# Expert gate and up products: weights become the stationary operand, 96 token slots stream, high and low halves lie side by side

## The chip, the core and the metric

The kernel runs as one launch on one core of a Trainium2 chip. The metric is the device time of that launch in microseconds (us). Below, PE is TensorE's matrix multiply, PEld its weight load, DVE VectorE, ACT ScalarE, POOL GpSimd, SP SyncE, whose queue issues the large transfers.

## The reference

Two transformer blocks over 256 tokens of 1024 features. The part that matters here is the last layer's mixture of experts: 8 experts of 3584 hidden features, the best two for each token.

```python
def moe_swiglu(t, router, w_gate, w_up, w_down):
    logits = (t @ router).astype(jnp.float32)
    top_logits, top_idx = lax.top_k(logits, TOP_K)
    gates = jax.nn.softmax(top_logits, axis=-1)
    combine = jnp.sum(jax.nn.one_hot(top_idx, N_EXPERTS, dtype=jnp.float32) * gates[..., None], axis=1)
    out = jnp.zeros_like(t)
    for e in range(N_EXPERTS):
        out = out + combine[:, e:e + 1].astype(t.dtype) * swiglu(t, w_gate[e], w_up[e], w_down[e])
    return out
```

`swiglu` is silu(t wg) * (t wu), then times wd. For the inputs that the reference draws, its own routing gives the 8 experts 67, 89, 50, 69, 56, 58, 78 and 45 tokens.

## The kernel before

Every f32 operand is split into a high part (rounded to float32r) and a low part (what is left), and a product is the sum of three matmuls: high by high, high by low, low by high (`mm3`, L522 to L524). `load_w` (L494) fetches a weight tile in transfers of 1 MB into buffers `wf`, 12 of them in rotation, and splits it in units of 128 x 1024: ACT casts the high part `wh` (L491), DVE subtracts to get the low part `wl` (L492). `wh` and `wl` have four buffers each.

`moe` (L1623) routes first: each token gets a slot among an expert's tokens, up to 128 slots, and `G` is the one-hot matrix from tokens to slots. `gather` (L1713) multiplies the tokens by `G` for two experts at a time and leaves `xh` and `xl`, features on partitions, 2 x 128 slots on the free axis. Then come 8 experts with 7 chunks of 512 hidden features each. A chunk is `gate_up` (L1761) and, one chunk later, `down` (L1779):

- `gate_up` makes two products, gate and up, with `tm`: the 128 slots are the stationary operand (a 128 x 128 piece of `xh` or `xl` for each of 8 feature tiles), and 512 weight columns stream. That is 2 x 8 x 3 = 48 matmuls of 512 columns, into PSUM tiles `mm` of one bank, four in rotation. ACT takes silu of the gate sums (L1767), DVE multiplies by the up sums (L1768). The result has slots on partitions; four transposes on PE (L1771) turn it, ACT and DVE split it into `eah` and `eal` (L1775, L1776).
- `down` streams 512 columns of wd against `eah` and `eal`, 4 x 2 x 3 = 24 matmuls, into two banks `dn` that accumulate over the expert's 7 chunks.

After an expert's last chunk `combine` (L1792) weights its rows and returns them to their tokens. `finish` then takes the final norm and writes the output. `overflow` (L1821) computes slots 128 and up again in a loop that is entered only when an expert has more than 128 tokens.

The order on each engine is set by a scheduler when the program is built. All of `wf`'s transfers are issued by SP, in the order in which the tiles are used.

Of the kernel before, what the change touches and what calls it, by code (L numbers as in the profile page):

```python
# [9 lines left out]
F32 = mybir.dt.float32  # L10
F32R = mybir.dt.float32r
AF = mybir.ActivationFunctionType
OP = mybir.AluOpType
# [10 lines left out]
MLA_STEPS = 1.4  # L24
MODS_F32 = (1,3,5)
# [123 lines left out]
class Rwkv:  # L149
    """The recurrent mixer: r, k, v, feature-major [P, 4, S] (two heads a tile); chunks of 64 tokens."""  # L150
# [26 lines left out]
    def decays(self):  # L177
        """Decay from the start of a chunk of 64 tokens: to the token (e0), to the one before it (e1), inverted (em)."""
# [21 lines left out]
    def removal(self):  # L200
        """Normalized removal key."""
# [12 lines left out]
    def keys(self):  # L214
        """k (1 + (a - 1) k_a); decayed removal and replacement keys."""
# [15 lines left out]
    def blocks(self):  # L231
        """Diagonal blocks of 16 x 16, to one block per partition."""
# [27 lines left out]
    def inverses(self):  # L260
        """Inverses of the diagonal blocks by forward substitution, and back to tokens on partitions."""
# [20 lines left out]
    def queries(self):  # L282
        """Decayed queries and keys; bonus."""
# [26 lines left out]
    def group(self, g, yt):  # L310
        """Heads 4g .. 4g + 3, all tokens; a generator of steps."""
# [12 lines left out]
        for tt in range(2):  # L324
# [3 lines left out]
            # token-major copies  # L328
# [15 lines left out]
            # inverse of the 64 x 64 blocks, transposed  # L344
# [38 lines left out]
            # the two chunks of 64 tokens  # L383
# [33 lines left out]
    def finish(self, j, yt):  # L417
        """Group norm, bonus, gate of head pair j."""
# [14 lines left out]
class Build:  # L433
# [60 lines left out]
    def load_w(self, src, kt, cols):  # L494
        """Loads and splits a weight tile [P, kt, cols]; a list of (k0, kn, hi, lo) units."""
# [30 lines left out]
    def fm(self, units, c0, act, t0, n, M=P):  # L526
        """Feature-major product: weight columns c0..c0+M on partitions, tokens t0.. on the free axis."""
# [7 lines left out]
    def side(self, ws, act, ns):  # L535
        """Feature-major products of several weight tiles side by side, so that each uses act as it comes."""
# [9 lines left out]
    def tm(self, units, c0, n, act, t0):  # L546
        """Token-major product: tokens t0..t0+127 on partitions, weight columns c0.. on the free axis."""
# [37 lines left out]
    def head_rstd(self, sq, n, eps, floor=None):  # L585
        """1/sqrt(sum of sq over the 64 features of a head + eps), [P, n] in PSUM, for sq of two heads."""
# [18 lines left out]
    def spread(self, out, cols):  # L605
        """Token-major columns as rows, the same on every partition."""
# [4 lines left out]
    def first_rstd(self, h):  # L611
        """The same of the two inputs, in SBUF, for a start with nothing else to do."""
# [11 lines left out]
    def modnorm(self, h, act, streams, gs, sh, rs=None, first=None):  # L624
        """act = split(rmsnorm(h)*gs + sh); gs, sh: per stream [P, KT] columns (sh None: no shift)."""
# [20 lines left out]
    # ------------------------------------------------------------------ block 1  # L646
# [25 lines left out]
    def mods(self, l, chunks, plain=()):  # L672
        """Modulation vectors of layer l, columns in chunks of 384, both streams, feature-major; one step a chunk."""
# [68 lines left out]
    def gains(self, l, which, name):  # L742
        """Per stream (norm gain * (1 + scale)) and shift columns."""
# [11 lines left out]
    def decay(self, l, h, cross):  # L755
        """Transposed decay matrix [keys, queries] of retention head h, keys and queries of one stream or across."""
# [19 lines left out]
    def softmax_pv(self, scores, nkt, vt, opart, ops, ocols):  # L776
        """scores: one [P queries, nkt*P keys] tile per query tile; o^T (64 rows) goes into ops."""
# [19 lines left out]
    def padded(self, src, par, n):  # L797
        """One head's rows of a head pair's [P, n] tile, the other head's rows zero."""
# [35 lines left out]
    def rot(self, ps, dst, scale):  # L834
        """dst = scale * rotary(ps) for a [P, S] tile of two heads' features."""
# [9 lines left out]
    def retention(self, l, hp, rq, rk, rv, gate, ns):  # L845
        """Head pair hp: normalized, gated output replaces gate."""
# [28 lines left out]
    def headnorm(self, ops, n, eps, narrow=False):  # L875
        """(y - mean) / sqrt(var + eps) per head of 64 features, of a [P, n] PSUM tile of two heads."""
# [21 lines left out]
    def neighborhood(self, l, hp, naq, nak, nav, out, ns):  # L898
        """Head pair hp: output goes to out."""
# [35 lines left out]
    def layer_a(self, l):  # L935
# [111 lines left out]
        # output projection, gated residual  # L1047
# [5 lines left out]
        # convolutional feed-forward  # L1053
# [16 lines left out]
        for half in range(2):  # L1070
# [9 lines left out]
            for ft in range(0, KT, 2):  # L1080
                # two tiles side by side at first, while the last products are split
# [10 lines left out]
    def conv(self, l, ps, f, ns):  # L1092
        """Depthwise convolution over tokens of one feature tile, with bias."""
# [24 lines left out]
    def raw(self):  # L1118
        """The next buffer for weights as they come: the weight pool's, then those that another pool adds."""
# [38 lines left out]
    def leave(self):  # L1158
        """Block 1's output hb = rmsnorm(h) * g, and 1/rms of hb (from the mean squares of h * g)."""
# [37 lines left out]
    # ------------------------------------------------------------------ block 2  # L1197
    def norm_into(self, dst, name, then=lambda k: None):
        """dst = rmsnorm(h) * gain, f32."""
        rs = self.rstd(self.h, KT, S, self.c("mean"), self.eps, 0)  # L1200
        for k in range(KT):
            self.nc.vector.scalar_tensor_tensor(dst[:, k, :S], self.h[:, k, :S], self.v(name, k), rs[:, :S],
# [3 lines left out]
    def attention(self, q, k, v, opart, ops, scale):  # L1206
        """Causal attention of one head over S tokens: q, k [rows, S] feature-major, v(kt) [P, 64] token-major."""
# [26 lines left out]
    def layer_b0(self, rs=None, enter=None, leave=None):  # L1234
# [78 lines left out]
        # the shared rotary key, once per quadrant  # L1313
# [22 lines left out]
    def last(self, g):  # L1336
        """Runs a generator to its end; its value."""
# [6 lines left out]
    def rounds(self, *parts):  # L1344
        """Steps of (generator, steps a round), interleaved until all have ended."""
# [10 lines left out]
    def out_proj(self, w_out, yt, k0):  # L1356
        """Adds the products of mixer outputs k0 .. k0 + 3 to h; a generator."""
# [34 lines left out]
    def rope(self, ps, swap, cos, sin, writes, scale=1.0):  # L1392
        """Rotary embedding of a [P, S] tile; writes: (destination, rows)."""
# [10 lines left out]
    def mla(self, wqn, wqr, wkv, ql, kvl, kpe, yt):  # L1404
# [26 lines left out]
        # heads 0, 1 of a group: rotary rows in 0-63, the rest in rows 64-127; heads 2, 3 the other way round  # L1431
# [39 lines left out]
    def layer_b1(self, rs):  # L1471
# [14 lines left out]
        # on the side where weights of the experts come early, once the first heads are done  # L1486
# [13 lines left out]
        # forget gates: inclusive cumulative log-sigmoid, one head per partition  # L1500
# [17 lines left out]
        # extra rows of a head's keys and queries: D[query] * 1 + 1 * (-D[key])  # L1518
# [29 lines left out]
        def pair(kt, q, k, v, scale):  # L1548
            """Attention of two heads, in step; their outputs split."""
# [38 lines left out]
        def routing(k):  # L1588
            """Squares and router logits of feature tile k, summed token-major; the norm's factor comes later."""
# [33 lines left out]
    def moe(self, sums, copies):  # L1623
# [30 lines left out]
        # token-major copies of the normalized tokens  # L1654
# [337 lines left out]
```

## Time and profile before

| what | value |
|---|---|
| time, median of 3 runs | 2738.32 us (2736.84 to 2741.67) |
| span of the profiled execution, from the first to the last instruction | 2735.8 us |
| the experts' stage in it, first product to last (1710.2 to 2715.2) | 1005 us |
| PE, DVE, ACT, POOL busy, share of the span | 97%, 73%, 60%, 7% |
| HBM read | 581.82 MB |

The profile is one execution, taken by the hardware profiler. It names instructions by line and by tiles, out<-in; a PE row's first tile after the arrow is the operand that streams. A matmul's row runs from its start to its modelled end, and successive matmuls overlap, so the distance between two starts says more than a duration. The profile gives no time for its own execution but the span, which lies 2.5 us below the median of the runs.

### The profile page before, as it was taken

What the parts mean: (1) busy time and instruction counts of PE and PEld (TensorE: products, weight loads), DVE (VectorE), ACT (ScalarE), POOL (GpSimd) and SP (SyncE); (2) the same over time, 40 slices, a digit from 0 to 9 for tenths busy, and PEclk for the clock granted to TensorE, in tenths of its full rate; (3) what the DMA queues carried; (4) which work ended last, traced back from release to release, by engine and by line L of the source; (5) the groups of instructions that cost most, each with busy time, mean ns of one, the idle gap of its engine ahead of it and who ended that gap; (6) DMA issues with size and microseconds to landing.
All of it is one profiled execution on the core that took longest, in us unless ns stands there. A gap on an engine that the chain in (4) does not pass through costs nothing.

```text
span 2735.8 us, 39494 instructions
## 1 busy us (share of the span) xinstructions
PE 2667.3 (97%) x14922; PEld 2206.9 (81%) x14922; DVE 1985.2 (73%) x2920; ACT 1632.5 (60%) x2459; POOL 202.7 (7%) x247
## 2 busy tenths in 40 slices
PE   7999999999999999999999999999999999999998
PEld 3866677888887799987899988888887787788776
DVE  5366668557455687675655568999989888888886
ACT  4365555334345665565444465877777777777775
POOL 0112100000112200222010100000000000000000
PEclk9999999999999999999999999999999999999998
DMA  7245245435241455531255546899999999999992
GB/s 260 74 149 173 86 130 193 133 130 167 93 134 47 129 180 192 168 122 25 86 174 197 182 140 238 309 367 353 326 358 346 362 334 364 343 360 332 365 345 100
DMA packets 113876, 585.93 MB, mean 214 GB/s; under 512 B 19537, under 2 KB 23137, under 8 KB 68753
## 3 DMA queue, kind: packets, MB, share of 16 engines
q1 hardware_dynamic: 111296, 575.57, 59.2%
q0 software_dynamic: 2384, 7.79, 1.1%
q8 instruction: 119, 1.95, 0.3%
q14 instruction: 77, 0.62, 0.1%
HBM read 581.82 MB, written 1.47 MB: 213 GB/s over the span
## 4 chain that ended last, share of the span: by engine, by line
PE 62%; DVE 2%; ACT 2%; DMA 1%; issue 1%; POOL 0%; DVEq 0%; ACTq 0%; SPq 0%; POOLq 0%
PE mm L523 14%; PE mm L522 14%; PE mm L524 14%; PE dn L522 4%; PE dn L523 4%; PE dn L524 4%; PE sm L169 1%; PE sm L1771 1%; DVE wl L492 1%; PE sm L1721 1%; ACT wh L491 0%; PE sm L1211 0%; DMA wf<-moe_wd 0%; PE sm L1227 0%; DMA wf<-ffn_wg 0%
## 5 line engine op out<-in xcount | busy, mean ns | idle before, releaser
L492 DVE TENSOR_TENSOR wl<-wf,wh 128x1024 fp32r<-128x1024 f32 (+3 forms) x1254 | 1288.5, 1056 | 396.8 <-ACT wh L491 387.2
L491 ACT CAST wh<-wf 128x1024 fp32r<-128x1024 f32 (+3 forms) x1254 | 1104.9, 907 | 587.9 <-PE mm L523 347.7
L522 PE MATMUL mm<-ah,wh 128*128 128x256 f32 (+1 forms) x1768 | 573.0, 328 | 12.3 <-ACT ah L642 5.9
L524 PE MATMUL mm<-ah,wl 128*128 128x256 f32 (+1 forms) x1768 | 571.4, 324 | 1.8 <-DVE wl L492 1.6
L523 PE MATMUL mm<-al,wh 128*128 128x256 f32 (+1 forms) x1768 | 570.2, 323 | 0.0
L522 PEld LDWEIGHTS mm<-ah,wh 128*128 128x128 f32 x1768 | 335.0, 191 | 46.3 <-ACT ah L642 7.0
L524 PEld LDWEIGHTS mm<-ah,wl 128*128 128x128 f32 x1768 | 336.6, 191 | 32.7 <-DVE wl L492 3.7
L523 PEld LDWEIGHTS mm<-al,wh 128*128 128x128 f32 x1768 | 337.2, 191 | 31.0 <-issue 4.6
L523 PE MATMUL mm<-wl,xh 128*128 128x512 f32 x896 | 358.1, 400 | 2.0 <-DVE wl L492 2.0
L522 PE MATMUL mm<-wh,xh 128*128 128x512 f32 x896 | 355.9, 397 | 0.0
L524 PE MATMUL mm<-wh,xl 128*128 128x512 f32 x896 | 353.5, 395 | 0.0
L523 PEld LDWEIGHTS mm<-wl,xh 128*128 128x128 f32 x896 | 168.5, 188 | 51.9 <-DVE wl L492 13.1
L522 PEld LDWEIGHTS mm<-wh,xh 128*128 128x128 f32 x896 | 168.6, 188 | 38.8
L524 PEld LDWEIGHTS mm<-wh,xl 128*128 128x128 f32 x896 | 168.4, 188 | 37.5
L524 PE MATMUL dn<-wh,eal 128*128 128x512 f32 x448 | 180.7, 403 | 0.0
L523 PE MATMUL dn<-wl,eah 128*128 128x512 f32 x448 | 177.7, 397 | 0.0
L522 PE MATMUL mm<-gh,wh 128*128 128x256 f32 (+1 forms) x528 | 169.2, 320 | 0.0
L523 PE MATMUL mm<-gl,wh 128*128 128x256 f32 (+1 forms) x528 | 169.1, 320 | 0.0
L524 PE MATMUL mm<-gh,wl 128*128 128x256 f32 (+1 forms) x528 | 169.1, 320 | 0.0
L522 PE MATMUL dn<-wh,eah 128*128 128x512 f32 x448 | 158.1, 397 | 0.0
L524 PEld LDWEIGHTS mm<-gh,wl 128*128 128x128 f32 x528 | 100.2, 190 | 8.0
L523 PEld LDWEIGHTS mm<-gl,wh 128*128 128x128 f32 x528 | 100.2, 190 | 7.9
(514 smaller groups left out, 3422.0 us busy)
## 6 DMA issues: line engine op xcount, KB each, us to landing
wf<-moe_wg SPq DMA_DIRECT2D x112, 1024.0 KB, 6.8
wf<-moe_wu SPq DMA_DIRECT2D x112, 1024.0 KB, 6.8
wf<-moe_wd SPq DMA_DIRECT2D x112, 1024.0 KB, 6.4
wf<-w_mod SPq DMA_DIRECT2D x64, 768.0 KB, 4.4
wf<-w_up SPq DMA_DIRECT2D x88, 512.0 KB, 3.5
wf<-w_down SPq DMA_DIRECT2D x32, 704.0 KB, 4.0
wf<-w_out SPq DMA_DIRECT2D x32, 512.0 KB, 3.9
wf<-w_qkg SPq DMA_DIRECT2D x30, 512.0 KB, 3.5
```

The source lines that it names most:

```text
L169: self.nc.tensor.matmul(o, l, r, start=True, stop=True)
L491: nc.scalar.copy(dh, src)
L492: nc.vector.tensor_tensor(dl, src, dh.bitcast(F32), op=OP.subtract)
L522: nc.tensor.matmul(out, lh, rh, start=first, stop=False)
L523: nc.tensor.matmul(out, lh, rl, start=False, stop=False)
L524: nc.tensor.matmul(out, ll, rh, start=False, stop=last)
L1721: nc.tensor.matmul(ps[:, m * S:m * S + S], src[:, tt, k * P:k * P + P], G[:, tt, e0:e0 + 2], start=tt == 0, stop=tt == 1)
L1771: nc.tensor.transpose(ps[:, j * P:j * P + P], s[:, j * P:j * P + P], self.c("ident"))
```

## The change

`SLOTS = 96` replaces 128 as the number of slots of an expert. In `gate_up` the operands change places: a 128 x 128 piece of the weights, `wh` or `wl`, is loaded as the stationary operand, and slots stream. `gather` now leaves one tile `xg` for each of the two experts, with 96 high columns and 96 low columns side by side, so a matmul with `wh` streams all 192 columns and one with `wl` the 96 high ones. The high and low sums are added afterwards (ACT copies one half, DVE adds the other). The sums have hidden features on partitions, so no transposes follow. A product's `mm` tile has two banks now, and there are two such tiles instead of four of one bank. `gather` for the next pair of experts is called at chunk 3 of the odd expert instead of its last chunk, into three `xg` buffers. `down` and `combine` are cut to 96 partitions. `overflow` runs for slots from 96 and from 224, each behind a test of its own.

```diff
-        self.psum((4, 2))
+        self.psum((2, 2))
...
         def gather(e0):
-            xh = self.mk(mp, [P, KT, S], F32R, "xh")
-            xl = self.mk(mp, [P, KT, S], F32R, "xl")
+            xs = [self.mk(mp, [P, KT, 2 * SLOTS], F32R, "xg", 3) for _ in range(2)]
+            n = 2 * SLOTS
             for k in range(KT):
                 ps = self.smps()
                 for m, src in enumerate((th, tl)):
                     for tt in range(2):
-                        nc.tensor.matmul(ps[:, m * S:m * S + S], src[:, tt, k * P:k * P + P], G[:, tt, e0:e0 + 2],
+                        nc.tensor.matmul(ps[:, m * n:m * n + n], src[:, tt, k * P:k * P + P], G[:, tt, e0:e0 + 2],
                                          start=tt == 0, stop=tt == 1)
-                nc.scalar.copy(xh[:, k], ps[:, :S])
-                nc.vector.tensor_copy(xl[:, k], ps[:, S:])
-            return xh, xl
+                v = ps[:, :2 * n].rearrange("p (m e c) -> p e m c", m=2, e=2)
+                for i, (x, copy) in enumerate(zip(xs, (nc.scalar.copy, nc.vector.tensor_copy))):
+                    copy(x[:, k].rearrange("p (m c) -> p m c", m=2), v[:, i])
+            return xs
...
-                a = self.gate_up(mp, e, ch, x, (e % 2) * P)
-                if e % 2 and ch == NC - 1 and e + 1 < E:
+                a = self.gate_up(mp, e, ch, x[e % 2])
+                if e % 2 and ch == 3 and e + 1 < E:
                     nx = gather(e + 1)
...
-    def gate_up(self, mp, e, ch, x, c0):
+    def gate_up(self, mp, e, ch, x):
         nc, I = self.nc, self.I
         TT = nc.vector.tensor_tensor
-        pg = [self.tm(self.load_w(I[n][e, ch], KT, 512), 0, 512, x, c0) for n in ("moe_wg_1_2", "moe_wu_1_2")]
-        s = self.t2k()
-        nc.scalar.activation(s, pg[0], AF.Silu)
-        TT(s, s, pg[1], op=OP.mult)
-        ps = self.smps()
-        for j in range(4):
-            nc.tensor.transpose(ps[:, j * P:j * P + P], s[:, j * P:j * P + P], self.c("ident"))
-        ah = self.mk(mp, [P, 4, P], F32R, "eah", 2)
-        al = self.mk(mp, [P, 4, P], F32R, "eal", 2)
-        p3 = ps.rearrange("p (j t) -> p j t", j=4)
-        nc.scalar.copy(ah, p3)
-        TT(al, p3, ah.bitcast(F32), op=OP.subtract)
+        n = 2 * SLOTS
+        sums = []
+        for name in ("moe_wg_1_2", "moe_wu_1_2"):
+            pg = self.mk(self.ps, [P, 2, 512], F32, "mm", 2)
+            for k0, kn, wh, wl in self.load_w(I[name][e, ch], KT, 512):
+                for i in range(kn):
+                    k = k0 + i
+                    for j in range(4):
+                        o = pg[:, j // 2, j % 2 * n:j % 2 * n + n]
+                        f = slice(j * P, j * P + P)
+                        nc.tensor.matmul(o, wh[:, i, f], x[:, k], start=k == 0 and j % 2 == 0, stop=False,
+                                         skip_group_check=True)
+                        nc.tensor.matmul(o[:, :SLOTS], wl[:, i, f], x[:, k, :SLOTS], start=False, stop=k == KT - 1,
+                                         skip_group_check=True)
+            v = pg[:, :, :2 * n].rearrange("p b (j h c) -> p b j h c", j=2, h=2)
+            t = self.t2k()[:, :4 * SLOTS]
+            t4 = t.rearrange("p (b j c) -> p b j c", b=2, j=2)
+            nc.scalar.copy(t4, v[:, :, :, 1])
+            TT(t4, v[:, :, :, 0], t4, op=OP.add)
+            if not sums:
+                nc.scalar.activation(t, t, AF.Silu)
+            sums.append(t)
+        s = sums[0]
+        TT(s, s, sums[1], op=OP.mult)
+        ah = self.mk(mp, [P, 4, SLOTS], F32R, "eah", 2)
+        al = self.mk(mp, [P, 4, SLOTS], F32R, "eal", 2)
+        s3 = s.rearrange("p (j t) -> p j t", j=4)
+        nc.scalar.copy(ah, s3)
+        TT(al, s3, ah.bitcast(F32), op=OP.subtract)
         return ah, al
...
     def overflow(self, mp, cnti, pos, sel, comb, th, tl, finish):
+        n = self.nc.values_load(cnti[0:1, 0:1], min_val=0, max_val=S)
+        for first in range(SLOTS, S, P):
+            self.overflow_part(mp, n, first, pos, sel, comb, th, tl, finish)
```

On PE, before, this stands where a chunk's down products end and the next chunk's gate product begins (a matmul's first name is where it adds, the two behind the arrow are the operands, the size is that of the result):

```order
L522 MATMUL dn_17099<-wh_17554,eah_17388 128x512
L523 MATMUL dn_17099<-wl_17555,eah_17388 128x512
L524 MATMUL dn_17099<-wh_17554,eal_17389 128x512
L522 MATMUL mm_17602<-wh_17584,xh_16799 128x512
L523 MATMUL mm_17602<-wl_17585,xh_16799 128x512
L524 MATMUL mm_17602<-wh_17584,xl_16800 128x512
```

And this stands at the same kind of place now:

```order
L523 MATMUL dn_18883<-wh_19636,eah_19332 96x512
L524 MATMUL dn_18883<-wl_19637,eah_19332 96x512
L525 MATMUL dn_18883<-wh_19636,eal_19333 96x512
L1779 MATMUL mm_19664<-xg_16800,wh_19667 128x192
L1781 MATMUL mm_19664<-xg_16800,wl_19668 128x96
L1779 MATMUL mm_19664<-xg_16800,wh_19667 128x192
L1781 MATMUL mm_19664<-xg_16800,wl_19668 128x96
L1779 MATMUL mm_19664<-xg_16800,wh_19667 128x192
L1781 MATMUL mm_19664<-xg_16800,wl_19668 128x96
```

Three matmuls of 512 columns for each of 8 feature tiles have become eight of 192 and 96 columns in turn, 64 for a product; the down products keep their count and their 512 columns, and the order of gate, up and down is kept.

On ACT, before, this stands where the gate sums of a chunk are read (`wh` rows are the casts of weights, the last four here those of a down tile):

```order
L491 CAST wh_18269<-wf_18263 128x1024
L1767 ACTIVATE t2k_18298<-mm_18228 128x512
L491 CAST wh_18312<-wf_18310 128x1024
L491 CAST wh_18316<-wf_18310 128x1024
L491 CAST wh_18322<-wf_18320 128x1024
L491 CAST wh_18326<-wf_18320 128x1024
```

And now, from the casts of the up tile to those of the next chunk's gate tile:

```order
L492 CAST wh_19540<-wf_19538 128x1024
L492 CAST wh_19544<-wf_19538 128x1024
L1786 COPY t2k_19523<-mm_19438 128x384
L1789 ACTIVATE t2k_19523<-t2k_19523 128x384
L492 CAST wh_19622<-wf_19620 128x1024
L492 CAST wh_19626<-wf_19620 128x1024
L492 CAST wh_19632<-wf_19630 128x1024
L492 CAST wh_19636<-wf_19630 128x1024
L1786 COPY t2k_19612<-mm_19527 128x384
L492 CAST wh_19667<-wf_19665 128x1024
```

The gate sums are still read behind the last cast of the up tile; what is new is a copy of the up sums, which stands behind the four casts of the down tile and ahead of the next gate tile's.

## Rows read from the trace of the kernel before

**Rows 1.** The page: busy engines; PE and granted clock in 40 slices of the span.
```profile
PE 2667.3 (97%) x14922; PEld 2206.9 (81%) x14922; DVE 1985.2 (73%) x2920; ACT 1632.5 (60%) x2459; POOL 202.7 (7%) x247
...
PE   7999999999999999999999999999999999999998
...
PEclk9999999999999999999999999999999999999998
```

**Rows 2.** Windows, the experts' stage: busy us (instructions) by engine, granted clock, DMA share, GB/s.
```profile
1710.20:2715.20 1005.00, 1002.98 (x4522) 805.77 (x4520) 889.76 (x885) 755.50 (x840) 0.00 (x0) 1.00 0.91 337
```

**Rows 3.** Chain that ended last, same stage: shares of its 1005 us by line.
```profile
by line: PE mm L523 21.0%; PE mm L522 20.5%; PE mm L524 20.5%; PE dn L522 10.2%; PE dn L523 10.2%; PE dn L524 10.2%; PE sm L1771 2.4%; PE sm L1721 1.5%; DVE wl L492 0.9%; DMA wf<-moe_wd 0.7%; PE sm L1816 0.5%; DVE hb L1819 0.4%; PE sm L1817
```

**Rows 4.** Groups by line and shape, same stage: count | busy us, mean ns | idle before.
```profile
L492 DVE TENSOR_TENSOR wl<-wf,wh 128x1024 fp32r<-128x1024 f32 x668 | 787.4, 1221 | 85.8 <-ACT wh L491 83.1
L491 ACT CAST wh<-wf 128x1024 fp32r<-128x1024 f32 x668 | 678.8, 1050 | 111.1 <-PE mm L524 81.6 <-PE dn L524 24.3 <-DVE wl L492 2.0
L523 PE MATMUL mm<-wl,xh 128*128 128x512 f32 x896 | 358.1, 400 | 2.0 <-DVE wl L492 2.0
...
L524 PE MATMUL dn<-wh,eal 128*128 128x512 f32 x448 | 180.7, 403 | 0.0
...
L1768 DVE TENSOR_TENSOR t2k<-t2k,mm 128x512 f32<-128x512 f32 x56 | 38.4, 686 | 21.5 <-PE mm L524 21.2
L1776 DVE TENSOR_TENSOR eal<-sm,eah 128x512 fp32r<-128x512 f32 x56 | 38.3, 683 | 0.0
...
L1767 ACT ACTIVATE t2k<-mm 128x512 f32<-128x512 f32 x56 | 33.3, 595 | 54.2 <-PE mm L524 54.2
L1775 ACT CAST eah<-sm 128x512 fp32r<-128x512 f32 x56 | 32.8, 585 | 66.3 <-PE sm L1771 66.1
```

**Rows 5.** Timeline of PE within a chunk (start us, us): first and last of ten.
```profile
2116.73 0.40 PE L522 MATMUL dn<-wh,eah 128*128 128x512 f32 x1
...
2118.83 0.40 PE L522 MATMUL mm<-wh,xh 128*128 128x512 f32 x1
```

**Rows 6.** Timeline, weight loads and their matmuls of one column, back to back, merged.
```profile
1152.08 1.87 PEld L1178 LDWEIGHTS sm<-ccom,t2k 128*128 128x128 f32 x16
...
1152.11 1.93 PE L1178 MATMUL sm<-ccom,t2k 128*128 128x1 f32 x16
...
2719.31 1.86 PEld L577 LDWEIGHTS sm<-ccom,t2k 128*128 128x128 f32 x16 [0.51 <-issue]
```

**Rows 7.** Timeline of weight loads about two matmuls of two columns, in the stage.
```profile
2096.60 0.41 PEld L1803 LDWEIGHTS sm<-comb,G 128*128 128x128 f32 x2
2096.94 0.19 PEld L522 LDWEIGHTS mm<-wh,xh 128*128 128x128 f32 x1
2097.05 0.19 PEld L523 LDWEIGHTS mm<-wl,xh 128*128 128x128 f32 x1
```

**Rows 8.** Timeline of PE in `combine`: matmuls of 256 columns back to back.
```profile
2099.39 0.28 PE L1817 MATMUL sm<-GT,yl 128*128 128x256 f32 x1
2099.51 0.28 PE L1816 MATMUL sm<-GT,yh 128*128 128x256 f32 x1
```

**Rows 9.** Windows: the one-column run of rows 6; a stretch at the lower clock.
```profile
1151.30:1153.80 2.50, 2.50 (x26) 2.50 (x24) 0.48 (x1) 0.81 (x2) 2.15 (x4) 1.00 0.30 91
...
1704.40:1711.10 6.70, 4.63 (x19) 4.37 (x20) 5.65 (x20) 1.85 (x4) 0.00 (x0) 0.50 0.35 137
```

**Rows 10.** Timeline of PE and PEld in that stretch at the lower clock.
```profile
1710.23 0.63 PE L522 MATMUL mm<-wh,xh 128*128 128x512 f32 x1
1710.66 0.63 PE L523 MATMUL mm<-wl,xh 128*128 128x512 f32 x1
...
1706.35 0.97 PEld L1675 LDWEIGHTS sm<-sel,cM 128*128 128x128 f32 x4
```

**Rows 11.** Waits from 1800 to 2600: who for whom, us, times, longest.
```profile
ACT wh L491 <- PE mm L524: 64.7, 156, 1.5
```

**Rows 12.** Timeline, the last transfers issued before the span's end at 2735.8.
```profile
2727.62 2.72 SPq L1754 DMA_DIRECT2D out_dram<-xh  x4
```

More of the change, by code (lines that the diff above doesn't have):

```diff
@@ L24 @@
 MLA_STEPS = 1.4
+SLOTS = 96
 MODS_F32 = (1,3,5)
@@ L1748, in moe @@
         self.combine(mp, prev[0], dn, G, comb, idr)
-        of = self.mk(mp, [P, KT, S], F32, "xh")
         out = I["out"].rearrange("(k p) t -> p k t", p=P)
         def finish():
-            self.norm_into(of, "final_norm_2", lambda k: k % 2 and nc.sync.dma_start(out=out[:, k - 1:k + 1], in_=of[:, k - 1:k + 1]))
+            of = [self.mk(mp, [P, 4, S], F32, t) for t in ("yh", "yl")]
+            self.norm_into(of, "final_norm_2", lambda k: k % 2 and nc.sync.dma_start(out=out[:, k - 1:k + 1], in_=of[k // 4][:, k % 4 - 1:k % 4 + 1]))
         finish()
@@ L1795, in combine @@
         TT = nc.vector.tensor_tensor
+        C = SLOTS
         gt = self.mk(mp, [P, S], F32R, "GT")
@@ L1798, in combine @@
         for tt in range(2):
-            nc.tensor.matmul(ps[:, tt * P:tt * P + P], G[:, tt, e], idr, start=True, stop=True)
-        nc.scalar.copy(gt, ps[:, :S])
+            nc.tensor.matmul(ps[:C, tt * P:tt * P + P], G[:, tt, e], idr, start=True, stop=True)
+        nc.scalar.copy(gt[:C], ps[:C, :S])
         ps = self.smps()
         for tt in range(2):
-            nc.tensor.matmul(ps[:, :2], G[:, tt, e], comb[:, tt, e], start=tt == 0, stop=tt == 1)
+            nc.tensor.matmul(ps[:C, :2], G[:, tt, e], comb[:, tt, e], start=tt == 0, stop=tt == 1)
         cs = self.mk(self.wk, [P, 1], F32, "cse", 2)
-        nc.vector.tensor_reduce(cs, ps[:, :2], axis=AX.X, op=OP.add)
+        nc.vector.tensor_reduce(cs[:C], ps[:C, :2], axis=AX.X, op=OP.add)
         yh = self.mk(mp, [P, D], F32R, "yh")
@@ L1809, in combine @@
             sl = slice(512 * hf, 512 * hf + 512)
-            nc.scalar.activation(yh[:, sl], dn[hf], AF.Copy, scale=cs)
-            nc.vector.scalar_tensor_tensor(yl[:, sl], dn[hf], cs, yh[:, sl].bitcast(F32), op0=OP.mult, op1=OP.subtract)
+            nc.scalar.activation(yh[:C, sl], dn[hf][:C], AF.Copy, scale=cs[:C])
+            nc.vector.scalar_tensor_tensor(yl[:C, sl], dn[hf][:C], cs[:C], yh[:C, sl].bitcast(F32),
+                                           op0=OP.mult, op1=OP.subtract)
         for k in range(0, KT, 2):
@@ L1815, in combine @@
                 f = slice((k + i) * P, (k + i) * P + P)
-                nc.tensor.matmul(ps[:, i * S:i * S + S], yh[:, f], gt, start=True, stop=False)
-                nc.tensor.matmul(ps[:, i * S:i * S + S], yl[:, f], gt, start=False, stop=True)
+                nc.tensor.matmul(ps[:, i * S:i * S + S], yh[:C, f], gt[:C], start=True, stop=False)
+                nc.tensor.matmul(ps[:, i * S:i * S + S], yl[:C, f], gt[:C], start=False, stop=True)
             hv = self.h[:, k:k + 2].rearrange("p a b -> p (a b)")
@@ L1821, in overflow, with overflow_part @@
     def overflow(self, mp, cnti, pos, sel, comb, th, tl, finish):
+        n = self.nc.values_load(cnti[0:1, 0:1], min_val=0, max_val=S)
+        for first in range(SLOTS, S, P):
+            self.overflow_part(mp, n, first, pos, sel, comb, th, tl, finish)
+    def overflow_part(self, mp, n, first, pos, sel, comb, th, tl, finish):
         nc, tc, I = self.nc, self.tc, self.I
         TT = nc.vector.tensor_tensor
-        rec = self.mk(self.dp, [P, 2, 8, 3], F32, "rec")
+        rec = self.mk(self.dp, [P, 2, 8, 3], F32, f"rec{first}")
         rs = self.mk(mp, [P, 2, 8, 3], F32, "recs")
-        nc.vector.tensor_scalar(rs[:, :, :, 0], pos, float(-P), None, op0=OP.add)
+        nc.vector.tensor_scalar(rs[:, :, :, 0], pos, float(-first), None, op0=OP.add)
         nc.vector.tensor_copy(rs[:, :, :, 1], sel)
@@ L1830, in overflow @@
         nc.sync.dma_start(out=rec, in_=rs)
-        n = nc.values_load(cnti[0:1, 0:1], min_val=0, max_val=S)
-        with tc.If(n > P):
+        with tc.If(n > first):
             with tc.For_i(0, 8, 1) as e:
```

12 lines of the change are left out of this document (6 added, 6 removed).

## The prediction, made before the run

> **What bounds the kernel now.** I read the page first. PE is busy for 97% of the span, full in the last 15 of the 40 slices, where the clock stays at its upper level [rows 1]. That is the experts' stage. Cut out by itself it is 1005 us, in which PE is busy 1003 us, DVE 890, ACT 756, the DMA engines 91%, with a granted clock of 1.00, the 2.4 GHz level [rows 2]. A busy PE alone proves nothing, since matmuls overlap, so the chain of waits decides: of the 1005 us, 62.0% go through the gate and up products (`mm`), 30.6% through the down products (`dn`), 2.4% through the transposes of L1771, and only 0.9% through DVE's split and 0.7% through a transfer [rows 3]. The waits say the same from the other side: ACT stands 64.7 us waiting until PE frees a `wh` buffer [rows 11]. So PE's own pace sets this stage; a PE cost added in it lands in the time nearly whole.
>
> Pace means the distance between starts. Ten matmuls of 512 columns start from 2116.73 to 2118.83, nine distances, so 0.2333 us each [rows 5], although each is listed as 0.40 us long [rows 4]. With it, 56 chunks x 48 = 2688 gate and up matmuls (896 in each of three groups) make 627 us, against 62.0% x 1005 = 623 in the chain; 56 x 24 = 1344 down matmuls make 314, against 308. The unit is right.
>
> **What is removed.** 627 us of gate and up matmuls and 2.4% x 1005 = 24 us of transposes: 651 us of PE.
>
> **What is added on PE.** Per product 8 feature tiles x 4 pieces x 2 = 64 matmuls, per chunk 128, in all 7168, each with its own 128 x 128 piece of weights to load: 2.7 times as many loads as before. Streaming would be cheap. At 0.2333 / 512 = 0.456 ns a column, 192 columns take 0.087 us and 96 take 0.044, together 0.131 us, and 3584 such pairs 471 us. But a matmul cannot run before its weights are in, and the trace shows what loads alone cost: where matmuls stream a single column, 16 loads of 128 x 128 take 1.87 us in one place and 1.86 in another, each load being listed as 0.19, so the distance is (1.87 - 0.19) / 15 = 0.112 and (1.86 - 0.19) / 15 = 0.111 us [rows 6]. The clock was 1.00 in that run [rows 9]. Those are f32 operands; for the split weights' own type I look behind the two-column matmuls of `combine`, where two loads of `xh` and `xl` pieces follow each other after 0.11 us [rows 7]. Both of the new shapes stream for less than that, so a load, not a stream, sets each of them. With 512 columns the load was hidden behind 0.233 us of streaming; that cover is what the change takes away. I take 0.111 us: 7168 x 0.111 = 796 us. The lower bound is rows 7's 0.110, 788 us; the upper is 0.12, the distance of 256-column matmuls, where load and stream are about equal [rows 8], 860 us.
>
> Here the Trainium skill speaks both ways, in TensorE: Matmul & The Clock Gate. Its section Back-to-back issue gap says that in a real stream of load and matmul pairs a matmul of 128 columns comes every 81 ns or so; by that the new matmuls would take 7168 x 0.081 = 581 us, less than the 651 removed. Its section on LDWEIGHTS puts a load at its columns over 1.2 GHz, 107 ns for 128, which would make 767 us. Rows 6 and 7 side with the second and are slower still by 3 to 5 ns; nothing in this trace shows the first for such operands.
>
> **Other PE work.** The down products keep 512 columns, so 96 instead of 128 stationary columns change nothing. `combine` is the same but for 96 partitions. `gather` has 128 matmuls, of 192 columns instead of 256: from 0.12 to 0.111, -1 us. That it is called earlier frees no one, as its 1.5% of the chain [rows 3] is work and not a wait.
>
> **DVE and ACT.** DVE loses a multiply and a subtraction of 512 columns (0.686 and 0.683 us) and gets four operations of 384. At 3/4 of those prices each is 0.51 us: +0.68 a chunk, +38 us over the stage. ACT loses 0.595 and 0.585 and gets four of some 0.44: +0.58 a chunk, +32 [rows 4]. DVE then has about 928 us of work and ACT 788 in a stage of some 1140. Both stay below PE, so I cost this at nothing; the cover is the 212 us that PE is longer than DVE. Two stalls that are in the chain now, 0.9% and 0.7%, together 16 us, should shrink, because a chunk gets 2.6 us longer while DVE's part gets 0.7 longer. I take half, -8; bounds 0 and -16.
>
> **Waits for `mm`.** Two tiles instead of four: a gate product cannot start until the last gate sums are read. Behind PE's last gate matmul stand on ACT the up tile's last cast (1.05 us) and the copy (0.44), and on DVE a split (1.22) and the addition (0.51): 3.2 us [rows 4], covered by the up product, 64 x 0.111 = 7.1 us. For up sums the same 3.2 us lie beside the down products, 24 x 0.2333 = 5.6 us. Nothing is added. While ACT waits for the sums, the next casts queue behind it; of four buffers three are ready then, 4 us or more of PE work.
>
> **The end.** A second test for overflow, after the output's last transfers. The last are issued by 2730.3, and the span ends 5.5 us later [rows 12]; the branch can cost between nothing and about that. I take 2.
>
> **The sum.** -651 + 796 - 1 - 8 + 2 = +138 us. The profiled span of 2735.8 becomes 2874; the median of the runs is 2.5 above the span, so 2876 us, slower by 5.0%.
>
> **Rivals.**
> *Loads hide after all (faster).* If the two loads of a pair cost no more than the streams, PE needs 471 us instead of 651. Its stage falls to 825, and DVE with 928 becomes the bound, the transfers with 0.91 x 1005 = 915 close behind. The stage would be some 965, the time about 2700. It decides the sign at 651 / 7168 = 0.091 us a matmul: below it the kernel is faster. The skill's 81 ns is such a case: PE would need 935 us, as much as DVE, and the time would again be about 2700. For it speaks that no row shows this exact stream of 96 and 192 columns; against it, that one-column matmuls, which have nothing to stream, come no faster than 0.111. 5%.
> *The sums are read too late (slower still).* If half of the products had to wait out the 3.2 us, that is 56 x 3.2 = 180 us more, 3056. It needs a delay beyond 7.1 or 5.6 us, and the built order puts the reads right behind four casts. 4%.
> *The clock falls.* The array streams fewer columns a second. At 0.50 [rows 9], the 1.2 GHz level, 512 columns came after 0.43 us and four loads took 0.97, about 0.22 each [rows 10]. Then 7168 x 0.22 + 1344 x 0.43 = 2155 instead of 1110 us, a time near 3920. Against it: PE would never stand idle, and the stretch of one-column matmuls kept 1.00 [rows 9]. 4%.
> *An expert overflows 96 slots*, and all the experts' weights (8 x 3 x 1024 x 3584 x 4 bytes, 352 MB) are fetched again, 1045 us at the stage's 337 GB/s [rows 2]. The reference's routing gives 89 at most. 1%.
> That the change does not do what it says is excluded by the built order, which has the 64 matmuls per product.
>
> **Numbers.** The forecast has 85%; its own range, from both ends of the load, the stalls and the branch, is 2738 + (788 - 651 - 1 - 16) = 2858 up to 2738 + (860 - 647 + 5) = 2956. I cut the top to 2925, since at 192 and 96 columns the stream is further below the load than in rows 8, and set the bottom at 2845 for a load 2 ns shorter than any row shows. That leaves out the faster rival, the top and the far slower ones, together not over 2 in 10. A change below 0.2% cannot be told from none here. Faster by more: 5%; within: 1%; slower: 94%.
>
> **What the new profile would show.** In the experts' stage PEld near 100% of the time in gate and up; starts of L1779 and L1781 about 0.111 us apart with little difference between them; a stage of about 1140 us; DVE and ACT below 85%; the DMA share down from 0.91 to about 0.80; the chain almost wholly PE; clock 1.00. I am wrong if L1781 starts 0.05 us behind L1779 (loads hide), if PE waits for ACT or DVE before a chunk's first L1779, or if the clock leaves 1.00.

## The result, and the profile after

| | before | after |
|---|---|---|
| time, median (range) | 2737.98 us (2736.84 to 2741.67, 4 runs) | 3040.45 us (3037.34 to 3044.15, 4 runs) |
| profiled span; mean granted clock | 2735.8 us; 0.987 | 3038.3 us; 0.939 |
| start of the span to the first gate product | 1710.2 us | 1713.2 us |
| the experts' stage, first product to last | 1004.9 us | 1299.9 us |
| in it: clock at 0.50; PE idle | 1.0 us; 2.0 us | 295.7 us in 11 stretches; 16.9 us |
| behind it | 20.7 us | 25.2 us |

The change makes the kernel slower, by a factor of 1.1104 (95% interval 1.1090 to 1.1119): 302 us, where 138 were forecast and 187 was the most that the range allowed. Lengths of stretches at either clock and PE's idle time are summed over the trace's own clock records and PE rows.

The profile's page of the changed kernel, to be set beside [rows 1], has PE as busy as before. What differs is the clock, which before was 9 in all of the last 15 slices but the very last:

```profile
PE 2950.4 (97%) x19178; PEld 2581.8 (85%) x19178; DVE 2036.4 (67%) x3035; ACT 1686.0 (55%) x2571; POOL 201.7 (7%) x247
...
PEclk9999999999999999999999789798979797989988
```

Windows of the changed kernel, with the columns of [rows 2]: the stage, a stretch of it at the upper clock, and one at the lower:

```profile
1713.20:3013.10 1299.90, 1282.97 (x8769) 1178.90 (x8768) 937.09 (x983) 806.33 (x948) 0.00 (x0) 0.89 0.74 261
1780.00:1899.00 119.00, 119.00 (x916) 109.10 (x916) 96.25 (x97) 84.46 (x98) 0.00 (x0) 1.00 0.90 316
1904.00:1933.00 29.00, 29.00 (x129) 27.83 (x129) 12.19 (x13) 10.05 (x12) 0.00 (x0) 0.50 0.39 135
```

PE looks full in both stretches, yet starts 7.7 matmuls per us in the first, which holds down products too, and 4.4 in the second; DVE, ACT and the transfers drop to about half with it. The stage is a mixture of the two. Its chain of waits is still mostly PE, with more than in [rows 3] of DVE's split (3.2% against 0.9%) and of `combine` (L1839 and L1840, 1.8%):

```profile
by line: PE mm L1779 48.4%; PE mm L1781 20.5%; PE dn L523 7.3%; PE dn L525 7.2%; PE dn L524 7.1%; DVE wl L493 3.2%; PE sm L1722 1.0%; PE sm L1840 1.0%; ACT wh L492 0.9%; issue 0.8%; PE sm L1839 0.8%; DVE t2k L1787 0.5%; DVE eal L1797 0.4%; 
```

The timeline of weight loads in gate and up, first at the clock 1.00, then at 0.50 (start us, us):

```profile
2204.84 0.19 PEld L1779 LDWEIGHTS mm<-xg,wh 128*128 128x128 f32 x1
2204.95 0.19 PEld L1781 LDWEIGHTS mm<-xg,wl 128*128 128x128 f32 x1
...
2206.40 0.19 PEld L1779 LDWEIGHTS mm<-xg,wh 128*128 128x128 f32 x1
...
1907.69 0.33 PEld L1779 LDWEIGHTS mm<-xg,wh 128*128 128x128 f32 x1
1907.90 0.33 PEld L1781 LDWEIGHTS mm<-xg,wl 128*128 128x128 f32 x1
...
1910.46 0.33 PEld L1781 LDWEIGHTS mm<-xg,wl 128*128 128x128 f32 x1
```

The first three rows are the ends of a run of 15 loads, the last three of one of 14. Fourteen distances in 1.56 us are 0.1114 us each at the upper clock, as forecast from [rows 6]; thirteen in 2.77 us are 0.213 at the lower, so a load slows with the clock. That the distance belongs to the load, and is not a fixed step of PE, shows in `combine`, whose loads for its two-column matmuls have 96 columns. The timeline at the upper clock:

```profile
1898.66 0.25 PEld L1825 LDWEIGHTS sm<-comb,G 128*96 128x96 f32 x2
1898.83 0.19 PEld L1779 LDWEIGHTS mm<-xg,wh 128*128 128x128 f32 x1
```

Two of them take 0.17 us until the next load starts, 0.085 each, where 96/128 of 0.1114 is 0.084.

What puts the clock down stands in the timeline of PE at the end of the first expert. It is one passage of seven such:

```profile
1898.72 0.28 PE L1825 MATMUL sm<-comb,G 128*96 128x2 f32 x2
1898.86 0.34 PE L1779 MATMUL mm<-xg,wh 128*128 128x192 f32 x1
...
1899.10 0.32 PE L1779 MATMUL mm<-xg,wh 128*128 128x192 f32 x1
1899.26 0.23 PE L1781 MATMUL mm<-xg,wl 128*128 128x96 f32 x1
1899.33 0.32 PE L1779 MATMUL mm<-xg,wh 128*128 128x192 f32 x1
...
1899.70 0.23 PE L1781 MATMUL mm<-xg,wl 128*128 128x96 f32 x1
1901.15 0.51 PE L1839 MATMUL sm<-GT,yh 96*128 96x256 f32 x2 [1.22 <-ACT yh L1832]
...
1905.64 0.49 PE L1779 MATMUL mm<-xg,wh 128*128 128x192 f32 x1
...
1929.53 0.70 PE L523 MATMUL dn<-wh,eah 128*96 128x512 f32 x1
...
1933.45 0.59 PE L523 MATMUL dn<-wh,eah 128*96 128x512 f32 x1
1933.87 0.40 PE L524 MATMUL dn<-wl,eah 128*96 128x512 f32 x1
```

After the last down product PE has eight thin matmuls, from 1898.86 to 1899.93, then stands idle 1.22 us until ACT has written `yh` (L1832) for `combine`. Before the change five, seven or eight matmuls of 512 columns stood there, depending on the expert, and PE did not stand idle. PE's timeline before, behind the third expert's last down product, where there are five:

```profile
2096.60 0.39 PE L524 MATMUL dn<-wh,eal 128*128 128x512 f32 x1
2096.83 0.28 PE L1803 MATMUL sm<-comb,G 128*128 128x2 f32 x2
2096.97 0.48 PE L522 MATMUL mm<-wh,xh 128*128 128x512 f32 x1
...
2098.22 0.40 PE L1816 MATMUL sm<-GT,yh 128*128 128x256 f32 x2
```

`yh` is late by the order on ACT and DVE too. The timelines of ACT and then of DVE in the changed kernel at this place, and last that of ACT in the kernel before, behind its third expert:

```profile
1898.83 1.05 ACT L492 CAST wh<-wf 128x1024 fp32r<-128x1024 f32 x1
1899.79 0.36 ACT L1822 CAST GT<-sm 96x256 fp32r<-96x256 f32 x1
1900.41 1.26 ACT L1832 ACTIVATE yh<-dn,cse 96x512 fp32r<-96x512 f32 x2 [0.26 <-DVE cse L1827]
```
```profile
1897.49 2.35 DVE L493 TENSOR_TENSOR wl<-wf,wh 128x1024 fp32r<-128x1024 f32 x2
...
1900.23 0.15 DVE L1827 TENSOR_REDUCE cse<-sm 96x1 f32<-96x2 f32 x1
```
```profile
2096.05 0.37 ACT L1800 CAST GT<-sm 128x256 fp32r<-128x256 f32 x1 [0.24 <-PE sm L1799]
2097.34 1.27 ACT L1810 ACTIVATE yh<-dn,cse 128x512 fp32r<-128x512 f32 x2 [0.92 <-DVE cse L1805]
```

Before, ACT stood ready 0.92 us ahead of `yh` here, and started it 0.3 us after PE's last down row ended; in the other experts of the stage the distance is 0.3 to 1.3 us. Now a weight cast and the cast of `GT` stand ahead of it on ACT, two weight splits and `eal` stand on DVE ahead of `cse`, for which `yh` waits last, and it starts 1.7 us after the last down row in all seven places.

The clock goes to 0.50 at 1903.13, stays there through nearly all of a chunk's gate and up products, and comes back at 1933.85, 4.3 us after the first down matmul. All seven waits in `combine` end so (six stretches of 30.7 us and one of 27.3); three passages through `gather`, which has down products around it, have a wait of 1.72 us and give 6.8 us each; and the stage begins with 63.6 us at 0.50. In all eleven stretches the clock rises 1.6 to 5.0 us after the first 512-column down matmul in it, and in none earlier. The timeline of PE at the first wait in `gather`:

```profile
1974.42 0.47 PE L1722 MATMUL sm<-G,th 128*128 128x192 f32 x2 [1.72 <-DVE xg L1727]
```

### The profile page after: what moved, and what is told of

The parts are those of the page before. It is cut to its first block, busy times and chain, and to the rows that moved or that the text cites. A ratio compares the mean times of both kernels' runs of the same rounds, so it can differ in the third digit from the quotient of the medians.

```text
span 3038.3 us, 48645 instructions
## 1 busy us (share of the span) xinstructions
PE 2950.4 (97%) x19178; PEld 2581.8 (85%) x19178; DVE 2036.4 (67%) x3035; ACT 1686.0 (55%) x2571; POOL 201.7 (7%) x247
## 4 chain that ended last, share of the span: by engine, by line
PE 63%; DVE 4%; ACT 2%; issue 1%; DMA 0%; POOL 0%; ACTq 0%; DVEq 0%; POOLq 0%; SPq 0%
PE mm L1779 21%; PE mm L1781 9%; PE mm L523 6%; PE mm L524 6%; PE mm L525 6%; PE dn L523 3%; PE dn L525 3%; PE dn L524 3%; DVE wl L493 2%; PE sm L170 1%; ACT wh L492 1%; PE sm L1722 0%; PE sm L1840 0%; PE sm L1839 0%; PE sm L1212 0%
## 5 line engine op out<-in xcount | busy, mean ns | idle before, releaser
L493 DVE TENSOR_TENSOR wl<-wf,wh 128x1024 fp32r<-128x1024 f32 (+3 forms) x1254 | 1306.6, 1057 | 651.2 <-ACT wh L492 641.5
L1779 PE MATMUL mm<-xg,wh 128*128 128x192 f32 x3584 | 911.5, 345 | 0.0
L1781 PE MATMUL mm<-xg,wl 128*128 128x96 f32 x3584 | 860.1, 245 | 0.0
L1779 PEld LDWEIGHTS mm<-xg,wh 128*128 128x128 f32 x3584 | 763.0, 213 | 3.2
L1781 PEld LDWEIGHTS mm<-xg,wl 128*128 128x128 f32 x3584 | 763.3, 213 | 2.1
L523 PE MATMUL dn<-wh,eah 128*96 128x512 f32 x448 | 184.7, 412 | 0.1
L525 PE MATMUL dn<-wh,eal 128*96 128x512 f32 x448 | 182.0, 407 | 0.1
L524 PE MATMUL dn<-wl,eah 128*96 128x512 f32 x448 | 181.7, 406 | 0.0
L523 PEld LDWEIGHTS mm<-gh,wh 128*128 128x128 f32 x528 | 100.0, 189 | 7.9
L525 PEld LDWEIGHTS dn<-wh,eal 128*96 128x96 f32 x448 | 75.5, 169 | 33.2 <-DVE eal L1797 0.2
```

The costliest lines, as they stand in the source:

```text
L493: nc.vector.tensor_tensor(dl, src, dh.bitcast(F32), op=OP.subtract)
L523: nc.tensor.matmul(out, lh, rh, start=first, stop=False)
L524: nc.tensor.matmul(out, lh, rl, start=False, stop=False)
L525: nc.tensor.matmul(out, ll, rh, start=False, stop=last)
L1779: nc.tensor.matmul(o, wh[:, i, f], x[:, k], start=k == 0 and j % 2 == 0, stop=False, skip_group_check=True)
L1781: nc.tensor.matmul(o[:, :SLOTS], wl[:, i, f], x[:, k, :SLOTS], start=False, stop=k == KT - 1, skip_group_check=True)
```

## The experiments

Theory A: a load sets the distance of the new matmuls, 0.111 us, and a wait of PE puts the clock down, where the thin matmuls, unlike 512-column ones, don't bring it back. Theory B: the thin matmuls put the clock down by themselves, wait or no wait. A third, S: their streaming, not their load, sets the pace. Each ratio is to the kernel before.

| run | what | time us | ratio (95%) | stage us | at 0.50 us | PE idle us |
|---|---|---|---|---|---|---|
| e1 | `combine` and `gather` moved | 2950.08 | 1.0770 (1.0752 to 1.0788) | 1207.2 | 104.2 | 18.2 |
| e2 | low matmuls 192 columns | 2934.36 | 1.0714 (1.0696 to 1.0732) | 1192.6 | 59.9 | 19.5 |
| e3 | 16 matmuls behind `combine` | 2984.23 | 1.0899 (1.0881 to 1.0917) | 1234.4 | 94.5 | 18.8 |
| e4 | gate and up as before | 2745.62 | 1.0035 (1.0020 to 1.0049) | 1001.1 | 5.6 | 10.5 |
| e5 | `combine` split, `gather` spread | 2912.59 | 1.0624 (1.0608 to 1.0641) | 1170.5 | 63.4 | 0.6 |
| e6 | e5 and 24 matmuls at the start | 2894.00 | 1.0561 (1.0544 to 1.0577) | 1138.2 | 0 | 0.2 |
| e7 | before, `yh` made 3 times | 2757.78 | 1.0061 (1.0046 to 1.0077) | 1017.9 | 1.4 | 9.0 |
| e8 | e4 with e5's edits | 2741.98 | 1.0009 (1.0000 to 1.0018) | 998.1 | 5.3 | 8.5 |
| e9 | before, `yh` made 7 times | 2793.24 | 1.0194 (1.0176 to 1.0212) | 1050.0 | 42.3 | 29.5 |
| e10 | e6 with e2's edit | 2893.85 | 1.0570 (1.0551 to 1.0589) | 1140.3 | 0 | 0.2 |

**e1.** `combine` is called behind the next chunk's gate and up products, and `gather` gives its pieces to chunks 2 to 5:

```diff
                 a = self.gate_up(mp, e, ch, x[e % 2])
...
+                if done is not None:
+                    self.combine(mp, *done, G, comb, idr)
+                    done = None
                 if prev is not None:
                     dn = self.down(dn, *prev, NC)
                     if prev[1] == NC - 1:
-                        self.combine(mp, prev[0], dn, G, comb, idr)
+                        done = (prev[0], dn)
```

> The change with its two stalls taken away by order alone: combine stands one chunk later, behind the next chunk's gate and up products, and gather is spread over chunks 2 to 5, two feature tiles in each. No work is added or left out. Theory A (a load sets each of the new matmuls, and a PE stall in combine or gather trips the clock, which the load-bound products then hold at 0.50 until down products come): after the stage's start the clock stays at 1.00; of the 297 us more at the lower clock, the 232 behind the start go, half of that is time, so about 3040 - 116 = 2924 us. Theory B (the thin streams lower the clock by themselves, stall or not): the clock falls as before, 3025 to 3045 us.

The edit missed half of its aim, and the time lies 26 us above the expected 2924. `gather`'s waits were gone, but `combine`'s grew, since its ACT and DVE work had moved with it. The timeline of PE in e1 shows why the kernel still gained 90 us:

```profile
1919.32 0.50 PE L1852 MATMUL sm<-GT,yh 96*128 96x256 f32 x2 [2.06 <-ACT yh L1845]
...
1921.88 0.63 PE L523 MATMUL dn<-wh,eah 128*96 128x512 f32 x1
...
1923.99 0.39 PE L525 MATMUL dn<-wh,eal 128*96 128x512 f32 x1
```

The wait is longer, 2.06 us, and the clock falls, but down products now follow and bring it back after 3.4 to 6.8 us instead of 30. So not the wait's length, but what PE does behind it, makes the 30 us.

**e2.** The low-weight matmuls stream all 192 columns, which adds the low by low term:

```diff
-                        nc.tensor.matmul(o[:, :SLOTS], wl[:, i, f], x[:, k, :SLOTS], start=False, stop=k == KT - 1,
+                        nc.tensor.matmul(o, wl[:, i, f], x[:, k], start=False, stop=k == KT - 1,
```

> The matmuls with the low weights stream all 192 columns instead of 96, which adds the low-by-low term. Same count of loads. Theory A (loads set the pace): at 1.00 the distance of both matmuls stays near 0.111 us, since 192 columns stream in 0.087; the time is no longer than 3040 us, and shorter if the fuller streams bring the clock back sooner. Rival (streams set the pace, loads hide): 3584 x 96 x 0.456 ns = 157 us more, 3197 us.

Streaming a third more columns of gate and up made the kernel 106 us faster than the changed one. S is out. The waits are no shorter (1.38 us in `combine`, 1.72 in `gather`), but two of the ten have no fall, the stretches at 0.50 shrink to 3.4 to 6.8 us, six of these eight with no down product in them, and the one at the stage's start shrinks from 71.7 to 17.1 (some 8 us of each lie ahead of the stage). With more columns behind the same loads the clock thus returned sooner.

**e3.** Sixteen useless matmuls of 512 columns behind every `combine`:

```diff
+        self.th = th
...
+        ps = self.smps()
+        for i in range(16):
+            nc.tensor.matmul(ps, idr, self.th[:, i % 2, :512], start=True, stop=True)
+        junk = self.mk(self.wk, [P, 1], F32, "junk", 2)
+        nc.vector.tensor_copy(junk, ps[:, :1])
```

> The change with 16 useless matmuls of 512 columns added behind each of the 8 combines (their sums go nowhere). They cost 8 x 16 x 0.2333 = 30 us at 1.00 and 55 us at 0.50. Theory A: dense columns right behind the stall bring the clock back before the load-bound products start, so stretches of about 30 us at 0.50 become some 10 us, about -80 us of lost time against +30 to 55: 2990 to 3015 us, faster with more work. Theory B: the clock stays low as before, 3070 to 3095 us.

With 30 us of PE work more (8 x 16 x 0.2333) it is 56 us faster than the changed kernel, 6 us below the expected range. Timeline and windows of e3:

```profile
2064.06 0.51 PE L1840 MATMUL sm<-GT,yh 96*128 96x256 f32 x2 [1.23 <-ACT yh L1833]
...
2068.13 3.95 PE L1846 MATMUL sm<-th,idr 128*128 128x512 f32 x16
```
```profile
1985.00:2270.00 285.00, 281.67 (x2146) 257.97 (x2146) 223.72 (x231) 192.56 (x223) 0.00 (x0) 1.00 0.86 301
```

The same wait of 1.23 us, and the clock stays at 1.00 over the 285 us that hold it and the next. Five of the seven `combine` waits have no fall any more, two have 6.8 and 3.4 us. So a wait of this length does not put the clock down by itself; the thin matmuls behind it have their part in the fall too.

**e4.** `gate_up` in the old orientation (slots stationary, 512 weight columns stream, transposes, four `mm` tiles of one bank), all other edits kept:

> All of the change except the new orientation: gate_up has slots stationary (96 high and 96 low columns in turn) and 512 weight columns streaming, three matmuls and transposes, with PSUM as before; 96 slots, the earlier gather, three xg tiles and the two overflow tests stay. Theory A and B alike: the loss lies in the orientation, so 2728 to 2745 us, the clock at 1.00 in the stage. Rival (the other edits cost something: the earlier gather, the second test): over 2760 us.

Nearly the whole loss lies in the orientation. The rest costs 0.35% (2745.62 us, where at most 2745 was expected); in the spans the end is 5.6 us longer than before. A row of PE's timeline, and the windows from the first rise of the clock to the last down product:

```profile
2153.01 0.47 PE L1722 MATMUL sm<-G,th 128*128 128x192 f32 x2 [1.20 <-DVE xg L1727]
```
```profile
1719.00:2714.40 995.40, 984.85 (x4492) 686.62 (x4490) 880.93 (x854) 748.49 (x828) 0.00 (x0) 1.00 0.91 340
```

A wait of 1.20 us, with 512-column products ahead of it and `gather`'s 192-column ones right behind, leaves the clock alone.

**e5, e6.** `combine`'s ACT and DVE work stays where it was, its matmuls come one chunk later, `gather` as in e1 (e5); e6 adds 24 useless matmuls of 512 columns ahead of the first gate product.

```diff
+                if done is not None:
+                    next(done, None)
+                    done = None
                 if prev is not None:
                     dn = self.down(dn, *prev, NC)
                     if prev[1] == NC - 1:
-                        self.combine(mp, prev[0], dn, G, comb, idr)
+                        done = self.combine(mp, prev[0], dn, G, comb, idr)
+                        next(done)
...
+        yield
         for k in range(0, KT, 2):
```

> The change with combine cut in two: its ACT and DVE part (yh, yl) stands right behind the expert's last down products, its products on PE one chunk later; gather is spread over four chunks. PE then has a whole chunk between the two parts. No work is added or left out. Theory A: no stall of over 0.5 us in combine or gather, so the clock stays at 1.00 from its first rise (near 1780) to the tail; the lower clock costs only the start, some 36 us; 2905 to 2920 us. Theory B (thin streams alone lower it): the clock falls in each expert as before, 2950 us or more.

> As e5, with 24 useless matmuls of 512 columns between the first gather and the first gate product, 22 of them in one run, to bring the clock up before the load-bound products begin. They cost about 10 us at 0.50. Theory A: the 72 us at 0.50 at the start shrink to under 20, -26 us against +5 to 10: some 2890 us. If the start is slow for another reason: 2915 to 2930 us.

Windows of e5 at the stage's start and over the rest of it, then of e6 over its stage:

```profile
1708.00:1779.50 71.50, 69.00 (x307) 66.70 (x308) 34.28 (x73) 27.15 (x40) 0.00 (x0) 0.50 0.36 119
1780.00:2886.60 1106.60, 1106.38 (x8484) 1013.08 (x8482) 903.06 (x944) 774.99 (x915) 0.00 (x0) 1.00 0.85 299
```
```profile
1727.90:2866.10 1138.20, 1137.97 (x8753) 1043.71 (x8751) 926.09 (x967) 796.38 (x941) 0.00 (x0) 1.00 0.84 298
```

This decides against B: the same 7168 thin matmuls, with no wait among them, run for 1138 us at 1.00. In e5 the only lower stretch is the start, where thin products follow PE's waits of the routing; with twenty-four wide matmuls (e6) it ends after 17 us, ahead of the first gate product.

**e7, e9.** The kernel before, with the copy that makes `yh` repeated, so that PE waits in `combine` with 512-column products around:

```diff
-            nc.scalar.activation(yh[:, sl], dn[hf], AF.Copy, scale=cs)
+            for _ in range(7):
+                nc.scalar.activation(yh[:, sl], dn[hf], AF.Copy, scale=cs)
```

> The kernel before, with combine's scaled copy on ACT (yh) made three times over, so that PE has to wait in combine; products stay 512 columns wide. Theory A: where the wait comes to over 1 us the clock falls, but the wide products bring it back within 7 us, so each of 8 combines costs the wait of 1 to 3 us and at most 3.5 us of clock: 2750 to 2785 us. Rival (a stall costs the same 30 us at the lower clock whatever follows): 8 x 17 more, 2870 us.

At three times the cover held nearly all of it: PE waited 0.37 us there, and the clock never fell, so e7 tells little. At seven:

> The kernel before with its weighted copy in combine made seven times instead of once, so that PE waits in every combine for longer than the 1.2 us of the changed kernel. At three times it cost 2.4 us an expert; four more copies of both halves at about 0.6 us each add 4.8 us, together 7.2 us an expert, 58 us, 2796 us. Theory A (a stall makes the clock fall anywhere, but only load-bound products keep it down): the clock may fall in combine, but the 512-column products that follow bring it back within 7 us each time: at most 8 x 3.4 us more, 2790 to 2825. Rival (a stall of that size costs 27 to 31 us at the lower level whatever follows): 8 x 15 us more, about 2915.

Timeline of PE in e9:

```profile
1858.86 0.80 PE L1817 MATMUL sm<-GT,yh 128*128 128x256 f32 x2 [2.89 <-ACT yh L1811]
...
1864.67 0.63 PE L523 MATMUL mm<-wl,xh 128*128 128x512 f32 x1
1865.09 0.57 PE L524 MATMUL mm<-wh,xl 128*128 128x512 f32 x1
1865.50 0.40 PE L522 MATMUL mm<-wh,xh 128*128 128x512 f32 x1
```

Waits of 2.87 to 5.00 us put the clock down here too, seven times, but for 3.4 to 6.8 us. With waits two to four times as long as the changed kernel's 1.22 us in `combine`, the clock stays down for less than a quarter of 30.7 us when wide matmuls follow.

**e8.** e4 with `combine` split and `gather` spread as in e5, to see whether the other edits, rid of their waits, beat the kernel before:

> The old orientation of e4 with the split combine and the spread gather of e5: e4's idle time of PE in gather (some 8 us) and after combine (some 5 us) goes, the longer end (some 5 us) stays. Both theories: 2730 to 2740 us, the same as the kernel before or up to 0.3% faster.

They don't: no difference by the 0.2% of the prediction, and 2 us above the expected range.

**e10.** e6 with the low-weight matmuls of e2:

> The kernel of e6 (no stalls in the stage), with the low-weight matmuls of gate and up streaming 192 columns instead of 96, so that the low by low term is added. Streamed columns of gate and up grow by a third at one and the same number of loads, at the full clock. Theory A (a load sets the distance of each matmul, 0.1115 us): within 15 us of e6, 2890 to 2910. Rival (streaming takes part in the pace): 3584 x 96 columns x 0.456 ns = 157 us more, about 3050.

The stage is 2 us longer with a third more columns. With the clock out of the way, this is the plainest measure that a load sets the distance and that the stream adds next to nothing.

## Why the prediction was wrong

**The load, right.** The step on which the sign hung, 0.111 us a matmul from one-column runs, is confirmed: 0.1114 in the trace, and e10 shows that streaming has no part in it. The stage without waits and clock falls is e6's 1138.2 us, against "some 1140"; over before that is +133, where -651 + 796 - 1 - 8 made +136. It is no luck of terms that cancel. Summed over the distances between PE's starts, gate and up take 797.6 us in e6 (796 forecast); before, they took 655.6 together with the transposes, 648 without the waits in them (651 forecast). Half of the expected look of it was off: matmul rows of a pair start 0.16 and 0.07 us apart, not evenly; their sum of 0.22 to 0.23 is two loads.

**The clock, wrong.** The step that failed is in the rival *The clock falls*, given 4%: "Against it: PE would never stand idle, and the stretch of one-column matmuls kept 1.00". PE stood idle 16.9 us, and the clock was at 0.50 for 295.7 us of the stage. The first half fell because of "`combine` is the same but for 96 partitions". Its matmuls are, but its cover is not: five to eight 512-column matmuls (5 x 0.2333 = 1.2 us to 8 x 0.2333 = 1.9) became eight thin ones (8 x 0.111 = 0.9 us), `yh`, whose making they hide, starts 1.7 us after the down products instead of 0.3 to 1.3, and PE waited 1.22 us. Likewise "That it is called earlier frees no one" looked for a gain only, and not for the wait of 1.72 us that PE now has in the middle of `gather` until DVE's cast to `xg` (L1727) frees its PSUM tile. The second half was true but not enough: the one-column run starts at the upper clock and shows that thin matmuls keep it, not that they bring it back. The rival's own price, 3920 us, was as wrong: it took the whole stage at 0.50, and 295.7 of 1299.9 us were.

**Where the 302 us went.** The spans differ by 302.5. The stage is 295.0 longer: 133 of load-bound work (e6 less before), 17 of PE's waits (16.9 - 0.2), and 145 left for the clock; by the distances of a load, 1 - 0.1114 / 0.213 = 0.48 of the 295.7 us at 0.50 would be 141. The stage's start comes 3.0 us later, not forecast, and the end is 4.5 us longer, not 2. Without the clock's 145 the time would be 2895, inside the range; e6, which removes the waits too but pays for 24 matmuls, has 2894.

**The stalls and the other engines.** "-8" meant the waits of before. Few of them show as idle time of PE (2.0 us in all), since a matmul's row ends after the next one could start. Taken as what the distances between PE's starts exceed their group's median by, where that is over 10 ns, waits are 12.5 us before and 3.5 in e6: -9, as forecast. In the changed kernel new ones came to 16.9 us of idle time, dearer by the clock. DVE at 72% and ACT at 62% of the stage stay below PE, as forecast (928 and 788 us of work were forecast, e6 has 926 and 796), and the `mm` tiles made no wait: PE waited in `combine` and `gather` almost alone.

**Two slips.** The top of the prediction's own range has 647 where 651 is removed; that makes it 2952 instead of 2956, and nothing hangs on it, as it was cut to 2925. Both loads of [rows 7] that are compared are of `xh`, not one of `xl`.

What stays open: the runs don't say how long a wait or how wide a matmul it takes; among wide matmuls nothing was tried between e4's wait of 1.20 us and e9's 2.87. Nor is it known why two of e3's seven waits in `combine` are followed by a fall and five are not. That gate and up with 96 stationary slots (e4) has a stage 4 us shorter than before's, with 8.5 us more of PE idle, was not followed up.

The Trainium skill has a like pattern, in TensorE: Matmul & The Clock Gate, section HAM oscillation: in a product of few rows a wait for a transfer stands behind every group of matmuls, and the next group starts at the lower clock each time; it advises to arrange the loop so that the groups stand together ahead of a wait, or to pad the rows. This case's trace agrees in that each of the seven waits in `combine`, 1.21 to 1.22 us long, is followed by a fall; but these waits were for ACT and DVE, and not for a transfer. A cure in the sense of the first is e5 (128 us back). The second was not run here; e2, with more columns for every other load and not more rows, gave 106 us back.

## What to carry to other kernels

Before making a weight tile stationary for a thin stream, price each matmul by its load from a run of one-column matmuls; that was right to 1%. Then look for every place where PE waits or would wait once the work beside it gets shorter: a wait of 1.2 us, harmless among wide matmuls (e4), cost some 15 us each among load-bound ones (half of 30.7), because the clock did not come back until wide ones ran. Splitting the waiting helper, so that its products come a chunk after the work that feeds them, took that away.

## What was not expected of the hardware

- The 7168 load-bound matmuls held 1.00 for 1138 us (e6), but after a fall in the changed kernel they did not regain it: up to 63.6 us of the stage at 0.50 until down products came. Wide products regained it within 6.8 us (e9).
- Streaming 192 instead of 96 columns behind every second load cost 2 us of stage (e10) and shortened the falls from about 30 to 6.8 us (e2): more work on PE for less time.
- A wait of 1.2 us is not enough for a fall: five of e3's seven (1.23 to 1.24 us, wide matmuls soon behind them) and both of e4's (1.20 us) left the clock at 1.00, and each of the changed kernel's seven was followed by one.
